# Order of the state products in the mLSTM part of a gated hybrid block, one Trainium2 core

## The chip, the core and the metric

The kernel runs on one core of one Trainium2 chip. A core has five engines with instruction queues of their own: TensorE (PE, the matrix engine, with a side called PEld that loads the stationary operand), VectorE (DVE), ScalarE (ACT), GpSimd (POOL) and SyncE (SP, which issues most transfers). Each engine takes its instructions in the order of the program; semaphores tie the engines together. The metric is the device time of one execution in microseconds (us), as the median of several runs.

## What is computed

One layer of a hybrid block over 2048 positions: a norm, a wide projection, three branches (mLSTM, gated linear attention called GLA, and a state-space branch called S5), gates, and an output projection. The change lies in the mLSTM branch, whose reference for one chunk of positions is this:

```python
def step(carry, inp):
    c_mat, n_vec, m = carry
    qt, kt, vt, it, ft = inp
    ...
    s = jnp.einsum('bhtd,bhsd->bhts', qt, kt) * w_intra
    num = (jnp.einsum('bhts,bhse->bhte', s, vt)
           + w_inter[..., None] * jnp.einsum('bhtd,bhde->bhte', qt, c_mat))
    den = jnp.sum(s, axis=-1) + w_inter * jnp.einsum('bhtd,bhd->bht', qt, n_vec)
    out = num / jnp.maximum(jnp.abs(den), jnp.exp(-m_t))[..., None]
    ...
    c_new = w_prev[..., None, None] * c_mat + jnp.einsum('bhs,bhsd,bhse->bhde', wk, kt, vt)
    n_new = w_prev[..., None] * n_vec + jnp.einsum('bhs,bhsd->bhd', wk, kt)
    return (c_new, n_new, m_new), out
```

Four heads of width 192 carry a state `c_mat` of 192 x 192 and a vector `n_vec`. For each chunk, q meets k (the scores) and q meets the state of the chunks before.

## The kernel before

The sequence is worked in 4 blocks of 512 positions (`NB`), each in 4 chunks of 128 (`NC`). In a block come `gla_pair` twice, `mlstm_gates`, `mlstm_pair` twice (a pair is two heads), then the gates, branches and `tail`. In block 0 the S5 branch (`s5_main`, lines 1015 to 1053) is woven into the part behind the mLSTM.

Nearly all of PE's work is dense products in `dense_fm` (lines 122 to 124, outputs of 512 columns) and `dense_tm` (lines 138 to 140, 384 columns). They work on a number format that needs one pass through the array; each matrix is split into a high and a low part, by ACT (line 85, `whi`) and DVE (line 86, `wlo`) or by ACT and POOL (lines 104 and 105). The products of the mLSTM chunks are in full 32-bit floats, which PE takes in two passes, so a row of the trace counts each of them as two instructions.

The loop over the chunks stands in `mlstm_pair`, lines 583 to 650; there are 4 x 2 x 4 = 32 chunks of two heads. The 2 x 192 rows of q and k lie in three tiles of 128 rows: `ma` holds 128 rows of the first head, `mc` 128 rows of the second, and `mb` 64 rows of each (`parts` at its head lists them). A product over the rows of `mb` so uses half of the rows of the array: rows 0 to 63 for the first head, rows 64 to 127 for the second. In the trace such an instruction has the mark 64*128, one over all rows 128*128. A chunk's steps:

- qk (line 590): two full-row and two half-row products, into the first 128 columns of two tiles `sp` in PSUM, one for each head.
- `wt` (lines 593 and 595): ACT makes the weights, DVE multiplies the scores with them.
- `ni` (line 599): `wt` times v.
- qC (line 603): q times the state (`C` in the code, `cst` in the trace), again two full-row and two half-row products, into columns 128 to 320 of the same two tiles `sp`.
- `num` (lines 606 and 607): ACT scales qC, DVE adds `ni`.
- `pkm` (line 611): transposes of k; `mkt` (line 615) on DVE; then `sa` and `sb` (lines 618 to 622) on PE and the update of the state on DVE (line 625).
- The rest norms the output (`num`, `sm`, `y`) and transposes it (`pty`, line 304).

The PSUM tiles of a chunk share three buffers (`psm`), so `pkm` takes the buffer of an `sp` tile once `num` has read that. The order of the instructions on each engine isn't that of the code alone: a scheduler that builds the program weaves the chunks with the dense products of what follows, by its own estimate of when things are ready.

Of the kernel before, what the change touches and what calls it, by code (L numbers as in the profile page):

```python
# [20 lines left out]
CH = 128  # L21
# [35 lines left out]
def hybrid_kernel(ctx: ExitStack, tc: tile.TileContext, a):  # L57
    nc = tc.nc
# [463 lines left out]
    def mlstm_pair(b, p, gates):  # L522
        ma, mb, mc = (mx.tile([128, 2, TB], F32, tag="b4", name="m" + i, bufs=B4) for i in "abc")
        q3 = [ma[:, 0, :], mb[:, 0, :], mc[:, 0, :]]
        k3 = [ma[:, 1, :], mb[:, 1, :], mc[:, 1, :]]
        parts = ((0, 128, 0), (0, 64, 1)), ((0, 128, 2), (64, 128, 1))
# [51 lines left out]
        C = cst[:, p]  # L578

        for c in range(NC):  # L580
            cs = slice(c * CH, (c + 1) * CH)
            v = vt[c]
            si = []
# [3 lines left out]
            for i in range(2):  # L587
                for j in range(2):
                    r0, r1, kk = parts[j][i]
                    nc.tensor.matmul(si[j][:, 0:CH], lhsT=k3[kk][r0:r1, cs], rhs=q3[kk][r0:r1, cs], start=(i == 0), stop=(i == 1))  # L590
            wt = mx.tile([128, 2, CH], F32, tag="wt", name="wt")
            for j in range(2):
                nc.scalar.activation(out=wt[:, j, :], in_=Mm[:, j, cs], func=AF.Exp, scale=-1.0,
# [3 lines left out]
            ni = psm.tile([128, 2, 193], F32, tag="m", name="ni")  # L597
            for j in range(2):
                nc.tensor.matmul(ni[:, j, :], lhsT=wt[:, j, :], rhs=v[:, j, :], start=True, stop=True)  # L599
            for i in range(2):  # L600
                for j in range(2):
                    r0, r1, kk = parts[j][i]
                    nc.tensor.matmul(si[j][:, CH:CH + 193], lhsT=q3[kk][r0:r1, cs], rhs=C[r0:r1, kk, :], start=(i == 0), stop=(i == 1))  # L603
            num = mx.tile([128, 2, 193], F32, tag="num", name="num")
            for j in range(2):
                nc.scalar.activation(out=num[:, j, :], in_=si[j][:, CH:CH + 193], func=AF.Copy, scale=tg[:, c, 1, h0 + j:h0 + j + 1])
# [133 lines left out]
    for b in range(NB):  # L740
        pool_lo[0] = True
        gla_pair(b, 0, gi)
        gla_pair(b, 1, gi)
        tg = mlstm_gates(b)
        mlstm_pair(b, 0, tg)
        mlstm_pair(b, 1, tg)
        pool_lo[0] = False
        acc = {}
        for i, bi in enumerate((1, 0, 2)):
            sg = [gate(bi, f) for f in range(2)]  # L750
            if i == (0 if b else 2):
                c_final(nc, a, mx, tl, b, dskip, u_d, y_d, z_d, y_a, dense_fm, split, full)
            if b == 0 and i == 2:
                gi = start(1)
            yl = {}
            for f in range(2):
                branch(b, acc, bi, f, sg[f], yl)
                if b == 0 and i < 2:
                    s5_steps(*(min(n5, -(-n5 // 4) * (2 * i + f + j)) for j in range(2)))
        if b and b + 1 < NB:  # L760
            gi = start(b + 1)
        tail(b, acc)
# [410 lines left out]
```

## Time and profile before

| | |
|---|---|
| median of 3 runs | 2981.83 us (2975.23 to 2982.64) |
| profiled execution, its own time | 2983.4 us |
| its span, first to last instruction | 2981.6 us |
| PE busy | 2854.9 us, 96% of the span |
| DVE, ACT, POOL busy | 58%, 42%, 31% |
| chunk loops of the mLSTM (blocks 0 to 3) | about 503 to 694, 1257 to 1445, 1912 to 2100, 2566 to 2755 us |
| S5 products on PE | 699 to 905 us |

The profile was taken of one execution, so sums from it stand against 2983.4 us. Start times in a timeline are given to 10 ns, and the time that an instruction takes of PE is the distance from its start to the next one's start, not its own duration: neighbours overlap in the array.

### The profile page before, as it was taken

The page shows a single profiled execution, that of the slowest core. Times are in us where ns is not written, and L with a number is a line of the kernel's source. Part 1 is how long each engine was busy: PE and PEld are TensorE (multiplying, and loading weights), DVE is VectorE, ACT ScalarE, POOL GpSimd, SP SyncE. Part 2 cuts the span into 40 slices and gives each one's busy share as a digit, 9 for nine tenths or more (in the row PEclk, how much of TensorE's full clock was granted, in tenths as well). Part 3 has the DMA queues.
Part 4 walks back from the last instruction along what each step waited for, and adds up shares of the span by engine and source line. Part 5 has one row for each costly group of instructions (what it writes and reads, how often), then busy time and mean ns, then how long its engine had stood idle before and what let it go on. Part 6 is the DMA issues. An engine that isn't in the chain of part 4 may idle for free. (4 is left out here: it accounts for less than half of the span.)

```text
span 2981.6 us, 41294 instructions
## 1 busy us (share of the span) xinstructions
PE 2854.9 (96%) x14360; PEld 2450.3 (82%) x14360; DVE 1740.8 (58%) x3289; ACT 1258.6 (42%) x2512; POOL 913.8 (31%) x783
## 2 busy tenths in 40 slices
PE   7898899999889999999999999999999999999998
PEld 7677889887667798988888798988888798898887
DVE  8766675645465666665434568565434658556335
ACT  4224444433224544444333644444334554444334
POOL 3453553212230345231122245231122344321022
PEclk9999999999999999999999999999999999999999
DMA  8665223335876332334444332324445332334433
GB/s 254 225 203 170 62 72 103 105 106 162 221 197 213 106 113 73 93 85 118 140 118 159 119 101 67 100 84 125 136 120 169 120 87 71 92 94 145 144 110 109
DMA packets 291442, 379.74 MB, mean 127 GB/s; under 512 B 83936, under 2 KB 194960, under 8 KB 288928
## 3 DMA queue, kind: packets, MB, share of 16 engines
q1 hardware_dynamic: 286112, 368.70, 41.9%
q10 hardware_dynamic: 5120, 8.39, 1.2%
q8 instruction: 113, 1.85, 0.3%
q14 instruction: 97, 0.79, 0.1%
HBM read 302.33 MB, written 65.04 MB: 123 GB/s over the span
## 5 line engine op out<-in xcount | busy, mean ns | idle before, releaser
L86 DVE TENSOR_TENSOR wlo<-raw,whi 128x512 fp32r<-128x512 f32 (+2 forms) x736 | 552.7, 755 | 776.1 <-ACT whi L85 651.5
L85 ACT CAST whi<-raw 128x512 fp32r<-128x512 f32 (+2 forms) x736 | 421.3, 576 | 715.3 <-PE d L123 429.5
L122 PE MATMUL d<-hn,whi 128*128 128x512 f32 x1472 | 590.1, 401 | 11.4 <-ACT whi L85 11.4
L123 PE MATMUL d<-hn,whi 128*128 128x512 f32 x1472 | 582.7, 396 | 0.0
L124 PE MATMUL d<-hn,wlo 128*128 128x512 f32 x1472 | 553.4, 398 | 6.5 <-DVE wlo L86 6.1
L139 PE MATMUL d<-wlo,hn 128*128 128x384 f32 (+1 forms) x1280 | 441.4, 345 | 13.7 <-DVE wlo L86 9.8
L140 PE MATMUL d<-whi,hn 128*128 128x384 f32 (+1 forms) x1280 | 434.3, 340 | 0.0
L105 POOL TENSOR_TENSOR wlo<-raw,whi 128x384 fp32r<-128x384 f32 x208 | 237.6, 1143 | 530.2 <-ACT whi L104 359.7
L138 PE MATMUL d<-whi,hn 128*128 128x384 f32 (+1 forms) x1280 | 387.0, 347 | 3.5 <-DVE zt L215 1.7
L122 PEld LDWEIGHTS d<-hn,whi 128*128 128x128 f32 x1472 | 279.6, 190 | 75.1 <-ACT whi L85 14.5
L124 PEld LDWEIGHTS d<-hn,wlo 128*128 128x128 f32 x1472 | 278.2, 190 | 70.6 <-DVE wlo L86 9.9
L123 PEld LDWEIGHTS d<-hn,whi 128*128 128x128 f32 x1472 | 279.5, 190 | 57.4 <-issue 0.9
L139 PEld LDWEIGHTS d<-wlo,hn 128*128 128x128 f32 x1280 | 242.4, 189 | 21.2 <-DVE wlo L86 12.8
L138 PEld LDWEIGHTS d<-whi,hn 128*128 128x128 f32 x1280 | 235.7, 189 | 12.9 <-issue 3.1
L140 PEld LDWEIGHTS d<-whi,hn 128*128 128x128 f32 x1280 | 242.6, 190 | 0.5 <-issue 0.2
L669 POOL TENSOR_TENSOR yl<-yraw,yl 128x512 fp32r<-128x512 f32 x64 | 84.4, 1320 | 444.6 <-ACT yl L668 422.1
L122 PE MATMUL d<-yl,whi 128*128 128x512 f32 x512 | 204.3, 400 | 3.6 <-DVE sg L674 1.9
L123 PE MATMUL d<-yl,whi 128*128 128x512 f32 x512 | 202.4, 395 | 0.0
L104 ACT CAST whi<-raw 128x384 fp32r<-128x384 f32 x208 | 106.2, 510 | 202.4 <-PE d L140 140.8
L124 PE MATMUL d<-yl,wlo 128*128 128x512 f32 x512 | 187.8, 395 | 3.8 <-DVE wlo L86 3.8
L679 POOL TENSOR_TENSOR sg<-sg 128x512 f32<-128x512 f32 x64 | 92.6, 1478 | 105.4 <-DVE sg L674 105.4
L539 DVE SCALAR_TENSOR_TENSOR cacc<-craw,convw,cacc 128x512 f32<-128x512 f32 x144 | 121.7, 845 | 2.7
(334 smaller groups left out, 4646.9 us busy)
## 6 DMA issues: line engine op xcount, KB each, us to landing
raw<-in_w_in_dram SPq DMA_DIRECT2D x480, 192.0 KB
raw<-in_w_in_dram SPq DMA_DIRECT2D x232, 256.0 KB
yraw<-y_a SPq DMA_DIRECT2D x64, 256.0 KB
raw<-in_w_out_dram SPq DMA_DIRECT2D x64, 256.0 KB
hnd<-hn SPq DMA_DIRECT2D x6, 2048.0 KB
y_a<-ys SPq DMA_DIRECT2D x64, 192.0 KB
raw<-in_w_bb_dram SPq DMA_DIRECT2D x48, 256.0 KB
raw<-in_w_ba_dram SPq DMA_DIRECT2D x48, 256.0 KB
```

What stands on the lines that cost most here:

```text
L85: nc.scalar.copy(out=hi, in_=src)
L86: nc.vector.tensor_tensor(out=lo, in0=src, in1=hi.bitcast(F32), op=ALU.subtract)
L104: nc.scalar.copy(out=hi[:, 0:n], in_=raw[:, 0:n])
L105: nc.gpsimd.tensor_tensor(out=lo[:, 0:n], in0=raw[:, 0:n], in1=hi[:, 0:n].bitcast(F32), op=ALU.subtract)
L122: nc.tensor.matmul(pm, lhsT=hi[:, o:o + mm], rhs=rh[:, ts], start=(k == 0), stop=False)
L123: nc.tensor.matmul(pm, lhsT=hi[:, o:o + mm], rhs=rl[:, ts], start=False, stop=False)
L124: nc.tensor.matmul(pm, lhsT=lo[:, o:o + mm], rhs=rh[:, ts], start=False, stop=(k == nk - 1))
L138: nc.tensor.matmul(ps[c][:, 0:n], lhsT=lh[:, cs], rhs=hi[:, 0:n], start=(k == 0), stop=False)
L139: nc.tensor.matmul(ps[c][:, 0:n], lhsT=lh[:, cs], rhs=lo[:, 0:n], start=False, stop=False)
L140: nc.tensor.matmul(ps[c][:, 0:n], lhsT=ll[:, cs], rhs=hi[:, 0:n], start=False, stop=(k == nk - 1))
L539: nc.vector.scalar_tensor_tensor(out=acc, in0=raw[:, i:TB + i], scalar=convw[:, t, i:i + 1], in1=acc, op0=ALU.mult, op1=ALU.add)
L679: nc.gpsimd.tensor_tensor(out=acc[i], in0=acc[i], in1=sg[m], op=ALU.add)
```

## The change

The four qC products move up to directly behind the four qk products of the same chunk, ahead of `wt` and `ni`, and their order is turned round: the two half-row ones come first, the two full-row ones behind them. So the half-row products of qk and qC follow each other. The number and the shapes of all instructions are the same. In the new kernel `wt` has the lines 597 and 599, `ni` line 603 and qC line 594; from line 604 on the numbers are the same.

```diff
@@ -588,6 +588,10 @@
                 for j in range(2):
                     r0, r1, kk = parts[j][i]
                     nc.tensor.matmul(si[j][:, 0:CH], lhsT=k3[kk][r0:r1, cs], rhs=q3[kk][r0:r1, cs], start=(i == 0), stop=(i == 1))
+            for i in (1, 0):
+                for j in range(2):
+                    r0, r1, kk = parts[j][i]
+                    nc.tensor.matmul(si[j][:, CH:CH + 193], lhsT=q3[kk][r0:r1, cs], rhs=C[r0:r1, kk, :], start=(i == 1), stop=(i == 0))
             wt = mx.tile([128, 2, CH], F32, tag="wt", name="wt")
             for j in range(2):
                 nc.scalar.activation(out=wt[:, j, :], in_=Mm[:, j, cs], func=AF.Exp, scale=-1.0,
@@ -597,10 +601,6 @@
             ni = psm.tile([128, 2, 193], F32, tag="m", name="ni")
             for j in range(2):
                 nc.tensor.matmul(ni[:, j, :], lhsT=wt[:, j, :], rhs=v[:, j, :], start=True, stop=True)
-            for i in range(2):
-                for j in range(2):
-                    r0, r1, kk = parts[j][i]
-                    nc.tensor.matmul(si[j][:, CH:CH + 193], lhsT=q3[kk][r0:r1, cs], rhs=C[r0:r1, kk, :], start=(i == 0), stop=(i == 1))
             num = mx.tile([128, 2, 193], F32, tag="num", name="num")
             for j in range(2):
                 nc.scalar.activation(out=num[:, j, :], in_=si[j][:, CH:CH + 193], func=AF.Copy, scale=tg[:, c, 1, h0 + j:h0 + j + 1])
```

The scheduler then orders the whole program anew. PE in the second chunk of block 0, before, around `ni` and qC (`mb` is the tile of the half-row products, `d` are dense products):

```order
L124 MATMUL d<-hn,wlo 128x512
L599 MATMUL ni<-v,wt 128x193
L603 MATMUL sp<-cst,ma 128x193
L603 MATMUL sp<-cst,mb 128x193
L599 MATMUL ni<-v,wt 128x193
L603 MATMUL sp<-cst,mc 128x193
L603 MATMUL sp<-cst,mb 128x193
L122 MATMUL d<-hn,whi 128x512
```

The same chunk after, from the qk products on:

```order
L304 MATMUL pty<-ident,y 128x128 x3
L590 MATMUL sp<-ma 128x128
L590 MATMUL sp<-mc 128x128
L590 MATMUL sp<-mb 128x128 x2
L594 MATMUL sp<-cst,mb 128x193 x2
L594 MATMUL sp<-cst,ma 128x193
L594 MATMUL sp<-cst,mc 128x193
L124 MATMUL d<-hn,wlo 128x512
```

Before, the two half-row qC products of this chunk are parted by other work; after, four half-row products stand in a row. PE in the fifth chunk of block 0 (the first of the second pair of heads), before, around the qk products:

```order
L140 MATMUL d<-whi,hn 128x384
L590 MATMUL sp<-ma 128x128
L590 MATMUL sp<-mc 128x128
L590 MATMUL sp<-mb 128x128
L138 MATMUL d<-whi,hn 128x384
L590 MATMUL sp<-mb 128x128
L139 MATMUL d<-wlo,hn 128x384
```

And after:

```order
L140 MATMUL d<-whi,hn 128x384
L590 MATMUL sp<-ma 128x128
L590 MATMUL sp<-mc 128x128
L590 MATMUL sp<-mb 128x128 x2
L138 MATMUL d<-whi,hn 128x384
L594 MATMUL sp<-cst,mb 128x193 x2
L594 MATMUL sp<-cst,ma 128x193
L139 MATMUL d<-wlo,hn 128x384
```

Here the half-row products of qk have come together, and those of qC too, but a dense product still parts the two pairs. Counted over the whole program, the half-row products on PE stand as follows before: qk 24 times as two in a row and 16 times alone, qC 20 times as two in a row and 24 times alone, which is 84 groups. After: 28 times four in a row (qk, qk, qC, qC), and 4 times two of qk and 4 times two of qC, which is 36 groups.

The third place is DVE in the first chunk of block 0. Before (`g` is another gate, `wlo` a split for dense products):

```order
L532 COPY craw<-hist 128x3
L563 SCALAR_TENSOR_TENSOR g<-tho,g 128x384
L595 SCALAR_TENSOR_TENSOR wt<-sp,wt 128x128
L563 SCALAR_TENSOR_TENSOR g<-tho,g 128x384
L595 SCALAR_TENSOR_TENSOR wt<-sp,wt 128x128
L86 TENSOR_TENSOR wlo<-raw,whi 128x384 x2
L607 TENSOR_TENSOR num<-ni,num 128x386
```

After:

```order
L532 COPY craw<-hist 128x3
L563 SCALAR_TENSOR_TENSOR g<-tho,g 128x384 x2
L86 TENSOR_TENSOR wlo<-raw,whi 128x384
L599 SCALAR_TENSOR_TENSOR wt<-sp,wt 128x128 x2
L86 TENSOR_TENSOR wlo<-raw,whi 128x384
L607 TENSOR_TENSOR num<-ni,num 128x386
L615 TENSOR_SCALAR mkt<-pkm,tg 128x192 x2
```

`wt` has moved behind one split and `mkt` up to right behind `num`. In the built program the semaphore for which `wt` waits is raised by the last half-row qk product before, and by the last qC product after; and `pkm` on PE stands right behind `ni` after, where dense products stood between them before. Outside the mLSTM chunks and what is woven with them (in block 0 the S5 part as well) the order of the engines is unchanged.

## Rows read from the trace of the kernel before

**Rows 1.** The page's first part: busy time (share of the span) and instructions, by engine.

```profile
PE 2854.9 (96%) x14360; PEld 2450.3 (82%) x14360; DVE 1740.8 (58%) x3289; ACT 1258.6 (42%) x2512; POOL 913.8 (31%) x783
```

**Rows 2.** Stretches: length, busy PE, PEld, DVE, ACT, POOL, PE clock, DMA share, GB/s.

```profile
500.00:690.00 190.00, 189.23 (x974) 160.12 (x973) 97.67 (x260) 79.08 (x175) 49.03 (x48) 1.00 0.38 108
1255.00:1445.00 190.00, 189.48 (x973) 160.24 (x972) 110.97 (x280) 85.75 (x187) 44.59 (x45) 1.00 0.39 108
690.00:940.00 250.00, 216.65 (x872) 170.25 (x871) 143.93 (x193) 71.11 (x127) 62.85 (x47) 0.94 0.74 205
```

**Rows 3.** PE's waits from 500 to 690 us: all of them (total us, times, longest).

```profile
PE d L139 <- POOL wlo L105: 0.8, 1, 0.8
```

**Rows 4.** Timeline of PE, first chunk, qk: start, us, line, tiles, array rows*columns, times.

```profile
504.51 0.34 PE L140 MATMUL d<-whi,hn 128*128 128x384 f32 x1
504.69 0.38 PE L590 MATMUL sp<-ma 128*128 128x128 f32 x2
504.91 0.39 PE L590 MATMUL sp<-mc 128*128 128x128 f32 x2
505.23 0.49 PE L590 MATMUL sp<-mb 64*128 64x128 f32 x4
505.65 0.50 PE L122 MATMUL d<-hn,whi 128*128 128x512 f32 x1
505.98 0.39 PE L123 MATMUL d<-hn,whi 128*128 128x512 f32 x1
506.21 0.40 PE L124 MATMUL d<-hn,wlo 128*128 128x512 f32 x1
```

**Rows 5.** Timeline of PE, first chunk, ni and qC.

```profile
510.79 0.49 PE L599 MATMUL ni<-v,wt 128*128 128x193 f32 x2
511.11 0.49 PE L603 MATMUL sp<-cst,ma 128*128 128x193 f32 x2
...
511.76 0.49 PE L603 MATMUL sp<-cst,mc 128*128 128x193 f32 x2
512.18 0.60 PE L603 MATMUL sp<-cst,mb 64*128 64x193 f32 x4
512.71 0.74 PE L124 MATMUL d<-hn,wlo 128*128 128x512 f32 x2
513.28 0.39 PE L122 MATMUL d<-hn,whi 128*128 128x512 f32 x1
```

**Rows 6.** Timeline of PE, second chunk, qC with its half-row products apart.

```profile
533.75 0.49 PE L603 MATMUL sp<-cst,ma 128*128 128x193 f32 x2
534.17 0.59 PE L603 MATMUL sp<-cst,mb 64*128 64x193 f32 x2
534.69 0.59 PE L599 MATMUL ni<-v,wt 128*128 128x193 f32 x2
535.12 0.49 PE L603 MATMUL sp<-cst,mc 128*128 128x193 f32 x2
```

**Rows 7.** Timeline of PE, third chunk, qk with its half-row products apart.

```profile
550.91 0.39 PE L590 MATMUL sp<-ma 128*128 128x128 f32 x2
551.23 0.48 PE L590 MATMUL sp<-mb 64*128 64x128 f32 x2
551.64 0.49 PE L590 MATMUL sp<-mc 128*128 128x128 f32 x2
552.06 0.49 PE L590 MATMUL sp<-mb 64*128 64x128 f32 x2
```

**Rows 8.** Timelines of DVE and PE: the second wt, the last sb, the last state update.

```profile
508.13 0.28 DVE L595 SCALAR_TENSOR_TENSOR wt<-sp,wt 128x128 f32<-128x128 f32 x1
...
523.47 0.33 PE L622 MATMUL sb<-v,mkt 128*64 128x193 f32 x1
...
524.02 0.41 DVE L625 SCALAR_TENSOR_TENSOR cst<-cst,wp,sb 128x193 f32<-128x193 f32 x1
```

**Rows 9.** PE's waits from 690 to 940 us, the three longest.

```profile
PE zp L1034 <- issue: 8.8, 5, 4.2
PE yp L1048 <- DVE uz L1029: 6.8, 5, 2.7
PE zp L1034 <- DMA mt<-mat_d: 4.4, 2, 4.0
```

## The prediction

> **What bounds the kernel now.** I read the page's busy times first: PE is busy for 96% of the span, no other engine for more than 58% [rows 1]. That is a mean over unlike stages, so I then read the stretches. In the stretches of the mLSTM chunks PE is busy for 189.2 of 190 us at full clock, DVE for 98 to 111, ACT for 79 to 86 [rows 2], and PE's waits there add up to 0.8 us [rows 3]. The chunks don't wait for anything: dense products fill every gap between their steps. So moving qC earlier shortens no wait of PE, since there is none. What can change is how much of PE's time the same products take. Behind the mLSTM of block 0, where the S5 part is woven in, it is different: PE is busy for 216.7 of 250 us, at a mean clock of 0.94 [rows 2], and waits in S5's products [rows 9].
>
> Last I read PE's timeline by distances from start to start. In a stream of full-row work a dense product of 512 columns takes 0.23 us (505.98 to 506.21), a qk product of two passes 0.22 (504.69 to 504.91) [rows 4], an `ni` or qC product 0.65 / 2 = 0.325 (511.11 to 511.76 holds two) [rows 5]. Around half-row products there is more:
>
> - Going in: `mc` to `mb` is 505.23 - 504.91 = 0.32, that is 0.10 over 0.22 [rows 4]; for qC 512.18 - 511.76 = 0.42, that is 0.095 over 0.325 [rows 5].
> - Inside: two half-row qk products take 0.42 (505.23 to 505.65) [rows 4], and one alone takes 0.41 (551.23 to 551.64) [rows 7]. For qC it is 0.53 for two (512.18 to 512.71) [rows 5] and 0.52 for one (534.17 to 534.69) [rows 6]. So two that stand together, on rows 0 to 63 and 64 to 127, run side by side: the second costs 0.01. A pass takes 0.42 / 2 = 0.21 against 0.11 in full-row work, so each half-row pass carries about 0.10 of its own.
> - Coming out: the first dense product behind takes 0.33 instead of 0.23 (505.65 to 505.98) [rows 4]; behind qC the two of line 124 take 0.57 instead of 0.46 [rows 5]; `ni` behind a lone qC half takes 0.43 instead of 0.325 [rows 6]. That is 0.10 to 0.11.
>
> A group costs, with its way in and out: two qk 0.10 + 0.42 + 0.10 = 0.62; one qk 0.10 + 0.41 + 0.10 = 0.61; two qC 0.095 + 0.53 + 0.11 = 0.735; one qC 0.095 + 0.52 + 0.105 = 0.72 us.
>
> **The change part by part.** The groups are counted in the two built programs (84 before, 36 after). Before, they take 24 x 0.62 + 16 x 0.61 + 20 x 0.735 + 24 x 0.72 = 14.9 + 9.8 + 14.7 + 17.3 = 56.6 us.
>
> 1. The parted qk halves come together: 16 lone ones become 8 pairs, 9.76 - 8 x 0.62 = 4.8 us less.
> 2. The parted qC halves come together: 24 become 12 pairs, 17.28 - 12 x 0.735 = 8.5 us less.
> 3. In 28 chunks the two pairs become one group. The trace has no such group. Its parts are 0.10 in, 0.42, 0.53 and 0.11 out, 1.16 us, if a qC pass behind a qk pass on the same rows carries the same 0.10 as a second qk pass does [rows 4]. One way out and one way in go: 0.62 + 0.735 - 1.16 = 0.195, x 28 = 5.5 us less. Bounds for the seam: it costs as much as leaving and coming back (nothing gained, 0 us), or it is free of the 0.10 as well (0.295 x 28 = 8.3 us). I take 5.5, since the seam is nearest to the step from pass to pass within a group: same rows, same mode of the array.
> 4. Four pairs of pairs stay parted by a dense product; they are in 1 and 2.
>
> Sum: 4.8 + 8.5 + 5.5 = 18.8 us, between 13.3 and 21.6. After, the groups take 28 x 1.16 + 4 x 0.62 + 4 x 0.735 = 37.9 us, which gives 18.7 the other way round.
>
> A rule of the Trainium skill bears on the seam. TensorEngine Tiling (Array Packing), Key Properties, says that changing the tiling mode, and not just the tile, drains the engine; the trace agrees that each change costs (0.10 in, 0.10 out). By that rule alone passes within the mode would be free of it, the seam too, and the sum would be 21.6; the trace shows 0.21 a pass within the mode [rows 4]. TensorE: Matmul & The Clock Gate, Part 3, says the opposite for the inside: a weight load runs under products in flight only where its row group differs. That fits the 0.10 of a half-row pass and would keep it at the seam, so 18.8.
>
> What else moves costs nothing, with these covers. **qC waits for the state.** It stands about 1 us behind the start of qk now. The last `sb` starts at 523.47, the state is written at 524.43 [rows 8], and the next chunk's first qC comes at 533.75 [rows 6]. In the new order more than 20 dense products of 0.23 us [rows 4] stand between `sb` and the next qk, some 5 us. **`pkm` behind `ni`** needs a PSUM buffer that `num` has read; ACT's `num` can now run during the dense products behind qC, before `ni`. **`wt`** waits for the last qC now: this is the first rival. **DVE, ACT, transfers** have the same instructions, and if PE's part of a block gets 4.7 us shorter in 190, DVE is still at 60%.
>
> Does the saving last to the end? In blocks 1 to 3 (14.1 us of it) PE is the bound through the chunks and nothing else paces them. In block 0 (4.7 us) the S5 part follows, where PE stands idle for 33 us in 250 [rows 2], so its share can be lost or doubled there.
>
> **The time.** 2983.4 - 18.7 = 2964.7 us for the profiled execution. That execution is 1.6 us over the median of the runs (2981.83), so for the median 2963 us, 0.63% less.
>
> **The rivals.**
>
> *`wt` is held, and PE after it (slower).* From the last half-row qk product to the last qC product PE needs 0.53 + 0.11 + 2 x 0.325 = 1.3 us, by which `wt` is released later in all 32 chunks. Behind `wt` on DVE wait the splits of line 86 that feed the dense products; behind `ni` on PE waits everything. Were nothing covered: 32 x 1.3 = 41.6, less 18.7: +22.9, so 3005 us. It decides from where the dense work between qC and `ni` gets shorter than two `wt` (0.56 us) and what DVE has before them; to lose what is gained, 0.6 us of every chunk must reach PE. Against it: `wt` ended at 508.41 and `ni` started at 510.79, 2.4 us spare [rows 5, 8], and in the tightest chunk of the new order 15 dense products of 384 columns, 0.17 to 0.18 us each [rows 4], stand between, 2.5 us or more. For it: DVE takes its work in order, and `wt` stands ahead of splits. 4%.
>
> *The S5 part of block 0 changes its waits.* The new order mixes its products otherwise with the dense ones. Waits of 20 us are named for three causes [rows 9]; I bound the effect by a third of the 33 us idle, 11 us either way: 2974 us (12%), or 2952 (6%).
>
> *The seam is free* (by the mode change being all that costs): 2.8 us more, 2960 us. 8%, since the passes within a group speak against it. It is the Trainium skill's rule on tiling modes (TensorEngine Tiling (Array Packing), Key Properties) taken alone.
>
> *The halves don't run side by side when four are queued:* 28 x 0.52 = 14.6 us are lost, 2978 us. The pairs of the trace all run side by side. 2%.
>
> **How the numbers follow.** The forecast, 2963, has 68%. A measurement of this kernel tells a difference from none at about 0.3%, so below 2972.9 counts as faster: forecast, free seam, the shorter S5 part and half of the longer one, 88%. Within 0.3%: the other half and the 2%, 8%. Slower: 4%. The range takes in the seam's bounds (2960 to 2969) and the S5 part either way: 2952 to 2975.
>
> **What would show it.** In the new profile: the group of four takes about 0.95 us from its first half-row start to the next full-row one; nearly all half-row pairs start together; a chunk stretch has no new waits for DVE's `wt` at `ni`; blocks 1 to 3 get 4 to 5 us shorter each. I am wrong if `ni` or the dense products wait for DVE there, or if 690 to 940 us changes by more than 10.

## The result and the profile after

The changed kernel takes 2942.09 us (median of 4 runs, 2935.25 to 2946.89) against 2979.77 us before: the ratio is 0.9872, with a 95% interval of 0.9857 to 0.9887, 37.7 us less. A second comparison, on another chip, gave 2948.44 against 2982.12 us, ratio 0.9883 (0.9868 to 0.9898). The forecast was 2963 us and a range of 2952 to 2975. The direction was right, but the size was half of what came, and the time lies outside the range.

The profiled execution took 2938.95 us. The page's busy times, and the stretches of the chunks of block 0 and of the S5 part (length, busy PE, PEld, DVE, ACT, POOL, then PE clock, DMA share and GB/s):

```profile
PE 2820.4 (96%) x14360; PEld 2435.3 (83%) x14360; DVE 1742.7 (59%) x3289; ACT 1254.5 (43%) x2512; POOL 910.3 (31%) x783
500.00:690.00 190.00, 189.54 (x1005) 163.56 (x1004) 103.67 (x268) 81.38 (x181) 49.11 (x48) 1.00 0.39 111
690.00:940.00 250.00, 224.13 (x969) 178.56 (x968) 147.92 (x220) 76.45 (x139) 63.84 (x47) 1.00 0.77 220
```

Against [rows 1, 2]: PE is as full as before in the chunks, and gets 1005 instructions done there instead of 974. From 690 to 940 us it gets 969 done instead of 872, and its clock there is 1.00 instead of 0.94. That second row is the half of the result that the forecast did not have.

The timeline of PE in the first chunk, after, answers to [rows 4, 5] (start, us, line, tiles, rows*columns of the array, times):

```profile
503.77 0.38 PE L590 MATMUL sp<-ma 128*128 128x128 f32 x2
503.99 0.39 PE L590 MATMUL sp<-mc 128*128 128x128 f32 x2
504.31 0.49 PE L590 MATMUL sp<-mb 64*128 64x128 f32 x4
504.63 0.49 PE L594 MATMUL sp<-cst,mb 64*128 64x193 f32 x4
505.06 0.59 PE L594 MATMUL sp<-cst,ma 128*128 128x193 f32 x2
505.49 0.49 PE L594 MATMUL sp<-cst,mc 128*128 128x193 f32 x2
```

The group of four takes 505.06 - 504.31 = 0.75 us inside. It goes in at 0.10 (0.32 from `mc` to `mb` instead of 0.22) and comes out at 0.10 (0.43 from `ma` to `mc` instead of 0.325): 0.95 in all, where the prediction had 1.16. Inside, from the first half-row start to the next full-row one, the prediction had 0.95, and it is 0.75 in all 28 groups of this trace. The two qk pairs take 0.32 of that, the two qC pairs 0.43, and this includes the switch back.

Where the time went, by starts in the two traces (the first qk product of a block, the last S5 product, the span):

```profile
L590 PE MATMUL sp<-ma x64: 271/275/276, 503.8 to 2690.1; 128*128 128x128 f32 x64
L1048 PE MATMUL yp<-uz,mt x64: 377/378/483, 706.9 to 879.4; 128*128 128x255 f32 x64
L590 PE MATMUL sp<-ma x48: 271/275/276, 1232.0 to 2690.1; 128*128 128x128 f32 x48
span 2937.2 us, 41314 instructions
```

The third line is the same query from 1200 us on, so that it begins in block 1. In the trace before, the same four points are 504.7, 904.7, 1258.6 and 2981.6 us.

| stretch | before | after | difference |
|---|---|---|---|
| start to the chunks of block 0 | 504.7 | 503.8 | -0.9 |
| chunks of block 0 and S5 part | 400.0 | 375.6 | -24.4 |
| behind it, to the chunks of block 1 | 353.9 | 352.6 | -1.3 |
| blocks 1 to 3, to the end | 1723.0 | 1705.2 | -17.8 |

So blocks 1 to 3 gave 17.8 us, nearly 6 each, and block 0 alone gave 24.4.

### The profile page after: what moved, and what is told of

The parts are those of the page before. It is cut to its first block, busy times and chain, and to the rows that moved or that the text cites. A ratio compares the mean times of both kernels' runs of the same rounds, so it can differ in the third digit from the quotient of the medians.

```text
span 2937.2 us, 41314 instructions
## 1 busy us (share of the span) xinstructions
PE 2820.4 (96%) x14360; PEld 2435.3 (83%) x14360; DVE 1742.7 (59%) x3289; ACT 1254.5 (43%) x2512; POOL 910.3 (31%) x783
## 5 line engine op out<-in xcount | busy, mean ns | idle before, releaser
L122 PE MATMUL d<-hn,whi 128*128 128x512 f32 x1472 | 586.8, 399 | 11.3 <-ACT whi L85 10.6
L539 DVE SCALAR_TENSOR_TENSOR cacc<-craw,convw,cacc 128x512 f32<-128x512 f32 x144 | 137.1, 952 | 2.7
```

The source lines that it names most:

```text
L122: nc.tensor.matmul(pm, lhsT=hi[:, o:o + mm], rhs=rh[:, ts], start=(k == 0), stop=False)
L539: nc.vector.scalar_tensor_tensor(out=acc, in0=raw[:, i:TB + i], scalar=convw[:, t, i:i + 1], in1=acc, op0=ALU.mult, op1=ALU.add)
```

## The experiments

After the result the theory was this. **A:** the groups of half-row products give 24.6 us over the whole program (56.6 - 28 x 0.95 - 4 x 0.62 - 4 x 0.735, the pairs at the prediction's prices), and the rest comes from the order in which the scheduler has put the S5 part of block 0. The rivals: **B**, the gain is spread over all blocks alike; **C**, the S5 part runs faster since PE comes to it earlier.

### The change in a part of the chunks

Five kernels take the new place of qC in some chunks and the old one in the others. The edit is one condition, here that of the smallest:

```diff
-            for i in (1, 0):
-                for j in range(2):
+            if b == 0 and p == 1 and c == 2:
+                for i in (1, 0):
+                    for j in range(2):
...
+            if not (b == 0 and p == 1 and c == 2):
+                for i in range(2):
+                    for j in range(2):
```

**Blocks 1 to 3 alone** (`b > 0`):

> qC directly behind qk in blocks 1 to 3 alone; block 0 is that of the kernel before, its S5 part too, instruction for instruction. By the new group costs (four in a row 0.95 us instead of 1.16) PE needs 18.4 us less for the half-row groups. Theory A (groups give 24.6 us in all, the rest of the gain comes from the order of the S5 part in block 0): 2980 - 18 = 2962 us, and the stretch from 690 to 940 us as in the kernel before. Rival B (the gain is spread over the four blocks alike, 37.7 / 4 = 9.4 each): 2952 us.

**Block 0 alone** (`b == 0`):

> qC directly behind qk in block 0 alone; its S5 part has the same order as in the changed kernel, blocks 1 to 3 that of the kernel before. Theory A: 6.1 us from the groups and some 13 from the S5 part, 2961 us. Rival B: 2970 us. If the new order of the S5 part is worth nothing: 2974 us.

**The second pair of heads of block 0** (`b == 0 and p == 1`):

> qC directly behind qk in the second pair of heads of block 0 alone, 4 chunks of 32. The groups give 3.0 us. The S5 part has the order of the changed kernel. Theory A (it is the order of the S5 part that gives the rest): 2980 - 3 - 13 = 2964 us, S5 part without stretches of low clock. Rival C (the S5 part runs faster because PE comes to it 12 us earlier): it comes some 3 us earlier here, so 2974 us or more.

**The first pair of heads of block 0** (`b == 0 and p == 0`):

> qC directly behind qk in the first pair of heads of block 0 alone. The groups give 3.5 us, and the S5 part gets a third order, neither that of the kernel before nor that of the changed kernel. If any order of the S5 part would have done as well as the changed kernel's: 16 to 20 us under the kernel before. If its gain belongs to that one order: 3.5 us, and the S5 part has its stretches of low clock again.

**One chunk of 32:**

> qC directly behind qk in a single chunk of 32 (block 0, second pair of heads, third chunk). The groups of half-row products give 0.4 us by that, but the scheduler gives the S5 part nearly the order that it has in the changed kernel (99 of 100 PE instructions there stand alike). Theory A (the order of the S5 part is worth 13 to 18 us by itself): 2982 - 14 = 2968 us. Theory C (the S5 part is faster because PE comes to it earlier): no difference that can be measured, 2982 us.

What was measured, each against the kernel before on its own chip:

| kernel | median | before | ratio and interval |
|---|---|---|---|
| blocks 1 to 3 | 2970.49 | 2982.96 | 0.9957 (0.9943 to 0.9972) |
| block 0 | 2967.00 | 2982.96 | 0.9947 (0.9929 to 0.9965) |
| block 0, second pair | 2966.21 | 2982.96 | 0.9944 (0.9923 to 0.9965) |
| block 0, first pair | 2970.55 | 2982.12 | 0.9962 (0.9947 to 0.9977) |
| one chunk | 2966.50 | 2984.75 | 0.9936 (0.9920 to 0.9953) |

One chunk of 32 moved, and the time fell by 18.3 us. Its half-row groups can have given 0.4 of that. Rival C is out. So is B: block 0 alone gives 16.0 us, where B had 10, and blocks 1 to 3 alone give 12.5, where B had 28. The kernel with the first pair fell between its two forecasts: 11.6 us, where it was to be 16 to 20 or 3.5. The stretch of the S5 part in the kernel with the one chunk, then in that with the first pair and in that with blocks 1 to 3 (three kernels, one row each):

```profile
690.00:940.00 250.00, 224.05 (x956) 178.06 (x955) 147.99 (x210) 75.84 (x138) 64.94 (x49) 0.99 0.78 219
```

```profile
690.00:940.00 250.00, 221.55 (x934) 178.08 (x933) 147.01 (x201) 75.05 (x136) 65.42 (x47) 0.97 0.76 216
```

```profile
690.00:940.00 250.00, 213.69 (x868) 166.69 (x865) 140.84 (x193) 69.52 (x124) 63.23 (x47) 0.95 0.73 200
```

With the S5 order of the changed kernel, or nearly, PE gets 956 done; with a third order 934; with that of the kernel before 868. The stretch from the first qk product of block 0 to the last S5 product, less what the groups gave, tells the same. The groups are counted in the built programs and priced as above; for the single pairs of heads that is 4.2 and 2.3 us, where the expectations had 3.5 and 3.0.

| kernel | S5 order | first qk to last S5, us | less than before | of it groups | left for the S5 order | PE clock, 690 to 940 us |
|---|---|---|---|---|---|---|
| before | old | 400.0 | | | | 0.94 |
| blocks 1 to 3 | old | 403.2 | -3.2 | 0 | -3.2 | 0.95 |
| block 0, first pair | a third | 386.1 | 13.9 | 4.2 | 9.7 | 0.97 |
| one chunk | nearly new | 385.1 | 14.9 | 0.4 | 14.5 | 0.99 |
| block 0, second pair | new | 379.5 | 20.5 | 2.3 | 18.2 | 1.00 |
| block 0 | new | 380.2 | 19.8 | 6.1 | 13.7 | 0.98 |
| changed kernel | new | 375.6 | 24.4 | 6.1 | 18.3 | 1.00 |
| changed kernel, second trace | new | 380.9 | 19.1 | 6.1 | 13.0 | 0.99 |

The new order is worth 13 to 18 us, and the clock says what the larger part of it is: a mean clock of 0.94 over 250 us is a loss of 15 us of full-clock time, 0.97 one of 7.5, 0.99 one of 2.5. In the trace of the kernel before one sees such a loss begin (PE's timeline, idle time before an instruction and its releaser in brackets):

```profile
718.11 0.70 PE L1048 MATMUL yp<-uz,mt 128*128 128x255 f32 x2 [2.71 <-DVE uz L1029]
...
719.33 0.99 PE L122 MATMUL d<-hn,whi 128*128 128x512 f32 x1
720.11 0.63 PE L123 MATMUL d<-hn,whi 128*128 128x512 f32 x1
720.54 0.63 PE L124 MATMUL d<-hn,wlo 128*128 128x512 f32 x1
720.97 0.63 PE L122 MATMUL d<-hn,whi 128*128 128x512 f32 x1
...
722.67 0.43 PE L123 MATMUL d<-hn,whi 128*128 128x512 f32 x1
722.94 0.39 PE L124 MATMUL d<-hn,wlo 128*128 128x512 f32 x1
```

PE waits 2.71 us for DVE, and then its dense products come 0.43 us apart (720.11 to 720.54) until 722.67; from 723 on they are 0.23 apart again. The granted clock from 719.2 to 722.6 us is 0.52, nearly all of it at the lower level, 1.2 GHz. The longest waits in the S5 part after the change:

```profile
PE yp L1048 <- DVE uz L1029: 7.8, 7, 2.1
PE zp L1034 <- issue: 4.0, 3, 1.8
PE d L124 <- DVE wlo L86: 3.9, 5, 1.3
PE zp L1034 <- DMA mt<-mat_d: 3.4, 4, 1.3
```

Against [rows 9] the single waits for DVE, for "issue" and for the DMA are 2.1, 1.8 and 1.3 us at the longest instead of 2.7, 4.2 and 4.0, and no stretch of low clock falls between 690 and 940 us. PE also waits less in sum. From the first qk product of block 0 to the last S5 product, before and then after (columns as above):

```profile
504.70:904.70 400.00, 368.94 (x1686) 300.46 (x1686) 219.12 (x417) 130.07 (x265) 108.44 (x92) 0.97 0.56 154
503.80:879.40 375.60, 352.15 (x1684) 288.97 (x1682) 215.75 (x417) 128.87 (x264) 109.87 (x92) 1.00 0.58 163
```

PE stands idle for 31.1 us before and for 23.4 after, 7.7 less, and a clock of 0.97 over 400 us is a loss of about 12 us, which is gone. With the 6.1 of the groups that makes 26, near the 24.4 by which the stretch became shorter (a wait at the low clock counts in both, and the clock is rounded). So of the 18 us some 12 are the clock's, as an estimate, and the rest are shorter waits. No kernel here held the waits and changed the clock alone, so no experiment shows this division.

Blocks 1 to 3 by themselves, from the first qk of block 1 to the end, in the kernel that changes them alone:

```profile
L590 PE MATMUL sp<-ma x48: 271/276/276, 1263.6 to 2721.5; 128*128 128x128 f32 x48
span 2968.7 us, 41306 instructions
```

2968.7 - 1263.6 = 1705.1 us, against 1723.0 before: 17.9 us, where the groups had 18.4. Its median fell by less, 12.5 us (8 to 17 by the interval), where A had 18: in the profiled execution the start, up to the first qk, took 508.1 us, 3.4 more than in the trace of before, and the stretch with the S5 part 3.2 more, though both are the same instructions in the same order. The start took 501.8 to 508.9 us in all kernels here; a few microseconds of each comparison are such scatter. The medians of the two halves, 12.5 and 16.0 us, add up to less than the 34 to 38 of the whole change, though their intervals reach it; their stretches in the traces, 17.9 and 19.8, do add up.

### The seam undone

```diff
-            for i in (1, 0):
+            for i in (0, 1):
...
-start=(i == 1), stop=(i == 0)
+start=(i == 0), stop=(i == 1)
```

> The changed kernel with qC directly behind qk, but its full-row products first, so that qk's and qC's half-row products are two groups again (32 pairs of qk, 28 pairs of qC and 8 lone ones); the S5 part has the changed kernel's order. Undoes term 3 of the prediction alone. With the group of four at 0.95 us (two fewer crossings at 0.2 each): 14 us more than the changed kernel, 2956 us. With the seam as the prediction had it (0.195 us a chunk): 8 us more, 2950 us. In its trace the pairs take 0.42 and 0.53 us again.

It took 2962.47 us against 2982.96, ratio 0.9933 (0.9913 to 0.9953): 20.5 us less than before, where the changed kernel is 34 to 38 less. So the seam is worth 13 to 17 us by the medians, nearer the 14 of the new price than the 8 of the prediction's. The medians come from different chips, and their intervals leave several microseconds either way, so they alone don't decide; the groups in the traces do. Its first chunk shows the two groups:

```profile
507.77 0.39 PE L590 MATMUL sp<-mc 128*128 128x128 f32 x2
508.08 0.49 PE L590 MATMUL sp<-mb 64*128 64x128 f32 x4
508.50 0.59 PE L594 MATMUL sp<-cst,ma 128*128 128x193 f32 x2
508.94 0.49 PE L594 MATMUL sp<-cst,mc 128*128 128x193 f32 x2
509.36 0.60 PE L594 MATMUL sp<-cst,mb 64*128 64x193 f32 x4
509.88 0.50 PE L122 MATMUL d<-hn,whi 128*128 128x512 f32 x1
```

0.42 and 0.52 inside, as in [rows 4, 5], and a way in and a way out for each.

In blocks 1 to 3 this kernel won only 3.7 us in its trace (1719.3 us from the first qk of block 1 to the end, instead of 1723.0), where the prices of its groups gave 7.8. PE's waits there add up to 26.5 us, 3.9 more than before, and the largest change is this one (the kernel before, then this one):

```profile
PE d L122 <- ACT whi L85: 4.6, 2, 2.3
PE d L122 <- ACT whi L85: 9.5, 5, 2.3
```

### A longer group

```diff
+            for j in range(2):
+                r0, r1, kk = parts[j][1]
+                nc.tensor.matmul(si[j][:, CH:CH + 193], lhsT=q3[kk][r0:r1, cs], rhs=C[r0:r1, kk, :], start=True, stop=True)
             for i in (1, 0):
```

> The changed kernel with one more pair of half-row qC products in each group, whose results are overwritten by the next: two passes of 193 columns more. If only the crossings between half-row and full-row work cost something, and passes within a group none: the group takes 0.75 + 2 x 0.163 = 1.08 us. If each pass had the 0.10 of the prediction: 0.95 + 2 x 0.263 = 1.48 us. The time is longer by the extra products, about 2948 + 15 = 2963 us, since further pairs are parted too.

It took 2958.21 us in one run. The group in its first chunk:

```profile
507.08 0.49 PE L590 MATMUL sp<-mb 64*128 64x128 f32 x4
507.40 0.49 PE L593 MATMUL sp<-cst,mb 64*128 64x193 f32 x4
507.73 0.49 PE L597 MATMUL sp<-cst,mb 64*128 64x193 f32 x4
```

The pair in the middle takes 507.73 - 507.40 = 0.33 us, two passes at 0.163, and the whole group 1.08. A pass inside a group costs nothing but its columns. The extra 0.1 falls at the crossings: once on the first pass behind one, once more on the pass behind that, on the way in and on the way out.

### The order within a group

```diff
...
             for j in range(2):
                 r0, r1, kk = parts[j][1]
                 nc.tensor.matmul(si[j][:, 0:CH], lhsT=k3[kk][r0:r1, cs], rhs=q3[kk][r0:r1, cs], start=False, stop=True)
+                nc.tensor.matmul(si[j][:, CH:CH + 193], lhsT=q3[kk][r0:r1, cs], rhs=C[r0:r1, kk, :], start=True, stop=False)
```

> The changed kernel with the four half-row products of a group in the order qk and qC of the first head, then qk and qC of the second. If PE starts products strictly in order, the second head's can run beside the last pass of the first head's alone: a group takes about 0.48 + 0.54 = 1.0 us instead of 0.75, some 7 us more in 28 chunks. If products on the other rows of the array are taken out of order: 0.75 us as before.

```profile
508.69 0.50 PE L592 MATMUL sp<-mb 64*128 64x128 f32 x4
509.01 0.50 PE L593 MATMUL sp<-cst,mb 64*128 64x193 f32 x4
509.44 0.59 PE L596 MATMUL sp<-cst,ma 128*128 128x193 f32 x2
```

The time was 2949.44 us in one run, within the 2940.50 to 2950.41 of the changed kernel on the same chip. All four qk passes (line 592, both heads) start before the first qC pass (line 593), though in the program the first head's qC stands ahead of the second head's qk; the group takes 0.75 us. PE starts half-row products on the other rows ahead of their turn: for these it is not so that an engine takes its instructions in the order of the program. So the halves need not alternate to run side by side; they only must not be parted by full-row work.

### The changed kernel again, and with sb brought together

> The changed kernel once more, beside the others of this group. By the stages of the two traces the groups give 24.6 us and the order of the S5 part 14 to 18 us: 38 to 42 us under the kernel before.

> The changed kernel with mkt of both heads made by one DVE instruction instead of two, so that the products sa and sb of both heads become ready together and all 32 pairs of sb (64 columns of the array each) stand together; 8 of 32 are parted now. From the trace a parted sb costs 0.09 + 0.47 + 0.10 = 0.67 us more than one in a pair: 8 x 0.67 = 5.4 us under the changed kernel, the S5 part unchanged in its order. If parted sb cost nothing, the same as the changed kernel.

```diff
-            for j in range(2):
-                js = slice(j * 192, (j + 1) * 192)
-                nc.vector.tensor_scalar(out=kt[:, js], in0=pk[:, js], scalar1=tg[:, c, 3, h0 + j:h0 + j + 1], scalar2=SC,
...
+            nc.vector.scalar_tensor_tensor(out=kt.rearrange("p (j d) -> p j d", j=2), in0=pk.rearrange("p (j d) -> p j d", j=2), scalar=SC,
+                                           in1=tg[:, c, 3, h0:h0 + 2].unsqueeze(2).to_broadcast([128, 2, 192]), op0=ALU.mult, op1=ALU.mult)
```

Beside each other on one chip: the changed kernel 2948.44 us (2940.50 to 2950.41), with one `mkt` 2940.86 (2936.99 to 2946.47), ratios 0.9883 and 0.9869 to the kernel before, with intervals that overlap. By the traces the 4.0 us that blocks 1 to 3 should have won are not there: from the first qk of block 1 to the end both take 1705 us (1705.1 and 1704.9). The products of `sb` stand together as meant, and new short waits of dense products stand against it (all of PE's waits there add up to 26.8 us, and to 23.6 in the changed kernel beside it), such as this one for ACT's splits in the chunks of block 1:

```profile
PE d L122 <- ACT whi L85: 1.6, 1, 1.6
```

So this expectation failed where it could be seen; whether the version is faster stays open.

## Why the prediction was right in direction and wrong in size

- **PE is the bound in the chunks and nothing new waits there:** right. PE's only wait from 500 to 690 us after the change is 0.5 us, for POOL, as in [rows 3]. The first rival, `wt` held by qC, did not show, though its cover was told wrongly: in the built program the fifth chunk of each block has only 4 dense products between the last qC and `ni`, not 15. PE has no wait at `ni` there all the same.
- **Parted halves come together, 4.8 and 8.5 us:** right. The kernel that has these two terms alone takes 46.2 us for its groups by the same prices, 10.4 less than before; it leaves 8 qC halves apart, worth 2.8. In blocks 1 to 3 it won 3.7 us instead of 7.8, and 3.9 us of new waits of PE stand against it: what PE saves in one place it can wait in another, which the prediction's sum did not have.
- **The seam, 5.5 us:** the step that failed is "so each half-row pass carries about 0.10 of its own". It was read from groups of two passes, where the second pass is also the one behind the crossing; those rows could not tell the two apart. The seam term measured 28 x (0.62 + 0.735 - 0.95) = 11.3 us, beyond its upper bound of 8.3, since that bound freed the seam and kept the 0.10 in the second qC pass. With it the groups give 24.6 us instead of 18.7. The Trainium skill says in TensorEngine Tiling (Array Packing), Key Properties, that changing the mode, and not just the tile, drains the engine; the traces agree in that each change costs 0.10 us twice, while passes within the mode cost their columns alone, 0.163 us. The Trainium skill's sentence in TensorE: Matmul & The Clock Gate, Part 3, that a weight load overlaps products in flight only where the row group differs, does not fit: passes on the same rows follow each other at 0.11 and 0.163 us, though each has a load of its own of 0.18 us.
- **The S5 part, 11 us either way, with 6% for the gain:** the mechanism was named, as a rival, and both its size and its chance were too small. The step that failed is "I bound the effect by a third of the 33 us idle, 11 us either way": it left the clock out, though 0.94 over 250 us stood in [rows 2] and is 15 us. The new order brought 13 to 18 us. The prediction's own sign of being wrong, more than 10 us in that part, came true.
- Together, 24.6 and 13 to 18 make 38 to 43 us; the medians show 34 to 38, with a start that scatters by 5 us.

## What to carry to other kernels

A price read from the shortest pattern hides which of its instructions pay; look for a longer run before a cost is put on each. Where a program's order is made by a scheduler, moving one step re-orders work far off, and a stage in which the bound engine waits and its clock falls has a gain or a loss of its own: price it by its waits and its clock loss, and measure it with an edit as small as one chunk.

## What the hardware showed

- A crossing between full-row and half-row products on PE costs about 0.1 us twice: 0.32 instead of 0.22 at the change and 0.21 instead of 0.11 at the next pass, and as much on the way back, 0.4 us for a group.
- Inside a group passes run at the rate of their columns (0.163 us for 193), and products on the other half of the rows are started ahead of earlier ones of the program (a group of 0.75 us in either order).
- After a wait of 2.71 us PE's granted clock was 0.52 from 719.2 to 722.6 us (1.2 GHz nearly throughout), with dense products 0.43 us apart instead of 0.23.
